# Up-projection of two ConvFFN layers: pairs of weight tiles by seven half-size products instead of eight, with sums of inputs and weights, and down groups added by DMA

## The chip, the cores and the metric

The kernel runs on one core of a Trainium2 chip. The metric is the device time of one execution in microseconds (us), lower is better. The engines are PE (TensorE), DVE (VectorE), ACT (ScalarE), POOL (GpSimd) and SP (SyncE, which issues DMA transfers). Each engine works through a row of instructions of its own, in a fixed order, and an instruction that waits holds up all that stands behind it in its row.

## The reference

Two layers over 528 tokens (16 meta tokens and 512 of the input) with 1024 features: sparse attention in the first, differential attention in the second, and after each a gated ConvFFN. The change lies in the ConvFFN:

```python
def conv_ffn(h, w_up, conv_w, conv_b, w_down):
    Tp = h.shape[1]
    u = h @ w_up
    up = jnp.pad(u, ((0, 0), (CONV_W - 1, 0), (0, 0)))
    c = conv_b + sum(up[:, j:j + Tp] * conv_w[j] for j in range(CONV_W))
    gate, val = jnp.split(c, 2, axis=-1)
    return (jax.nn.silu(gate) * val) @ w_down
...
h = h + conv_ffn(rms_norm(h, ln_ffn_g[i]), w_up[i], conv_w[i], conv_b[i], w_down[i])
```

`w_up` is 1024 x 5632 and `w_down` is 2816 x 1024. The 2816 columns of the gate and of the value half make 22 tiles of 128 each.

## The kernel before

Activations lie transposed, features on partitions and tokens along the row. Every fp32 product is made of three matmuls on numbers split into a high and a low part (fp32r): high by high, high by low, low by high. So a weight tile of 1024 x 128 arrives by DMA as `raw`, ACT casts it to `hi` (L111), and DVE (or POOL) subtracts to get `lo` (L113). The class `Weights` keeps one stream of such units, with three buffers each of `raw`, `hi` and `lo`; a unit's buffers come free when its matmuls are done.

`ffn(l)` runs over the tile pairs f = 0 to 21. For each f it makes the gate tile (e = 0) and the value tile (e = 1) with `lin`: 8 blocks of 128 features, two halves of the tokens (272 and 256; 260 and 256 in the second layer), three matmuls each, 48 matmuls to a tile, into one of two wide PSUM buffers (tag `sp`, two banks each). `evac` then does the convolution: ACT writes the first tap plus bias (L1065), DVE adds the two others (L1068, twice), ACT takes silu of the gate (L1073), DVE multiplies with the value (L1074), and ACT and DVE split the product into `ah` and `al` (L1077, L1078).

After pairs 6, 12 and 17 and at the end, `down` multiplies the finished act tiles with `w_down`, in eight groups (one for each 128 output features), and DVE adds each group's PSUM to the residual `h` (L1116). The order of instructions on each engine is set by a scheduler from the order of the code, the dependences and its own estimates.

Of the kernel before, what the change touches and what calls it, by code (L numbers as in the profile page):

```python
# [66 lines left out]
class Weights:  # L67
# [1 line left out]

    RAW = 3
    RING = 3

    def __init__(self, nc, pool, par):
        self.nc, self.pool, self.par = nc, pool, par
        self.units, self.loads, self.raw, self.out = [], [], {}, {}
        self.loaded = self.scaled = self.ready = self.taken = self.freed = 0
        self.held = 0

    def add(self, src, n=8, m=128, g=None, lo="v", fold=None):
        self.units.append((n, m, lo))
        self.loads.append((src, n, m, g, fold))

    def load(self):
        src, n, m, g, fold = self.loads[self.loaded]
        raw = self.pool.tile([128, 8, 128], F32, tag="raw", name="raw", bufs=self.RAW)
        dst = raw[:, :n, :m]
        self.nc.sync.dma_start(dst if fold is None else dst.rearrange("p (a k) c -> p a k c", a=fold), src)
        self.raw[self.loaded] = raw  # L90
        self.loaded += 1

    def scale(self):
        src, n, m, g, fold = self.loads[self.scaled]
        if g is not None:
            r = self.raw[self.scaled][:, :n, :m]
            self.nc.gpsimd.tensor_tensor(r, r, self.par[:, g:g + n, None].to_broadcast([128, n, m]), op=OP.mult)  # L97
        self.scaled += 1

    def split(self):  # L100
        nc = self.nc
        n, m, lo = self.units[self.ready]
        raw = self.raw.pop(self.ready)
        self.freed += 1
        r = raw[:, :n, :m]
        hi = self.pool.tile([128, 8, 128], F32R, tag="hi", name="hi", bufs=self.RING)
        lt = self.pool.tile([128, 8, 128], F32R, tag="lo", name="lo", bufs=self.RING)
        if lo == "pp":
            nc.gpsimd.tensor_scalar(hi[:, :n, :m], r, 1.0, 1.0, op0=OP.mult, op1=OP.mult)
        else:  # L110
            nc.scalar.copy(hi[:, :n, :m], r)  # L111
        eng = nc.vector if lo == "v" else nc.gpsimd
        eng.tensor_tensor(lt[:, :n, :m], r, hi[:, :n, :m].bitcast(F32), op=OP.subtract)  # L113
        self.out[self.ready] = (hi, lt)
        self.held += 1
        self.ready += 1

    def can_split(self):
        return self.ready < self.scaled and self.held < self.RING

    def pump(self, stop=None):
        while stop is None or self.ready < stop:
            if self.loaded < min(len(self.loads), self.freed + self.RAW):
                self.load()
            elif self.scaled < self.loaded:
                self.scale()
            elif self.can_split():
                self.split()
            else:
                return  # L130

    def take(self):
# [6 lines left out]
        return w  # L139

    def done(self):
        self.held -= 1
        self.pump()


# [4 lines left out]
class Trunk:  # L150
# [76 lines left out]
    def lin(self, x, evac, n=8, m=128, start=0, halves=(0, 1), w=None, kw=0, kx=0, done=True, tag="sp"):  # L227
# [9 lines left out]
        if done:  # L237
            self.wt.done()

    def halves(self, name):  # L240
        return tuple(self.ps.tile([128, 512], F32, tag="one", name=name) for _ in range(2))

# [9 lines left out]
    def setup(self):  # L252
# [15 lines left out]
        self.wt = Weights(nc, self.W, par)  # L268
        self.plan_weights()
        def part(s, k):  # L270
            c = slice(HO[s], HO[s] + HN[s])
# [60 lines left out]
    PW = ((0,0),(0,1),(1,0))  # L332

    def plan_ffn(self, l):
        wu, wd = self.a["w_up"][l], self.a["w_down"][l]
        for f in range(NF):
            for e in range(2):
                self.wt.add(wu[f + NF * e], lo=('p' if (f, e) in self.PW else 'v'))
            for f0, f1 in self.PARTS:
                if f == (f1 if f1 < NF else NF - 1):  # L340
                    for m in range(KC):
                        self.wt.add(wd[m][:, f0:f1, :], n=f1 - f0, lo="vv"[m % 2])

    def table(self, func, after=None):

# [133 lines left out]
    def norm(self, tmp, s, dst, g=None, start=0, gap=1.0, keep=None, lo="vp"):  # L479
# [23 lines left out]
        def apply(r):  # L503
            R = ps.tile([128, 512], F32, tag="one", name="R")
            for c in range(nt):
                i = nc.tensor.transpose(R[:, c * w:(c + 1) * w], r[:w, 8 + 2 * c:9 + 2 * c].to_broadcast([w, 128]),
                                        self.ident[:w, :w])
            self.hold(i)
            self.pe(0.107 * nt)
            dst[s] = self.xtile(s)  # L510
            xh, xl = dst[s][:2]
            o = c0 - HO[s]
            xfs, self.mults, self.his = [], [], []

            def low(m):
                eng = nc.vector if lo[m % len(lo)] == "v" else nc.gpsimd
                i = eng.tensor_tensor(xl[:, m, o:o + n], xfs[m][:, :n], xh[:, m, o:o + n].bitcast(F32),  # L517
                                      op=OP.subtract)
                if eng is nc.vector:
                    chain(i)  # L520

            last = [None]
# [527 lines left out]
    def ffn(self, l):  # L1050
# [1 line left out]
        st0 = 0 if l == 0 else 12  # L1052
        t0 = 0 if l == 0 else NM
        n = T - t0
        wt, x = self.wt, self.next_x
        cb = C_CONV + l * 176
        cnt = [0]
        self.xx, self.tm = ("ah", 8), ("c1", 2)
        with self.pool("fp") as fp:
            acts, conv = {}, {}  # L1060
            def evac(u, f, e, off=240):
                j = f + NF * e
                w0, w1, w2, b = (par[:, cb + 44 * q + j:cb + 44 * q + j + 1] for q in range(4))
# [24 lines left out]
            self.run(self.lin_many(x, first[2:], 0))  # L1088
            for j, (out, *_) in enumerate(first):
                if isinstance(out, tuple):  # L1090
                    u = fp.tile([128, T], F32, tag="uv", name="u", bufs=2)
# [25 lines left out]
                    if squares:  # L1117
                        self.norm_sum(fp, int(c0 == 272), m)

            def down(f0, f1):  # L1120
                last = f1 == NF
                squares = last and l == 0
                nf = f1 - f0

                def new():
                    cnt[0] += 1
                    if cnt[0] % 2:
                        t = ps.tile([128, 1024], F32, tag="sp", name="dn")
                    elif l == 1:
                        t = ps.tile([128, 512], F32, tag="one", name="dn")  # L1130
                    else:
                        t = self.halves("dn")
                    return t, wt.take()

                groups = [(0, 1), (2,), (3,), (4,), (5,), (6, 7)] if last else [(m,) for m in range(KC)]
                for grp in groups:
                    tw = [new() for _ in grp]
# [7 lines left out]
                    for ci, cc in enumerate(passes):  # L1145
# [2 lines left out]
                                block(t, w, f0 + k, k, cc, k == 0, k == nf - 1)  # L1148
                        for (t, w), m in zip(tw, grp):
                            add(t, m, cc, squares)  # L1150
                            if l == 1 and last:
# [10 lines left out]

            if l == 0:
                self.next_x = [None, None]
            for f in range(1, NF):
                for e in range(2):
                    if (f, e) != (1, 0):
                        self.run(self.lin(x, lambda u, f=f, e=e: evac(u, f, e), start=st0, tag="sp"))
                for f0, f1 in self.PARTS[:-1]:
                    if f == f1:  # L1170
                        down(f0, f1)
            if l == 0:
                self.table(AF.Sqrt, conv[0][:, 0:1])
            down(*self.PARTS[-1])
            self.flush()

# [469 lines left out]
```

## Time and profile before

| what | us |
|---|---|
| median of 3 runs (1385.61 to 1390.95) | 1386.35 |
| the profiled execution: its own time | 1384.77 |
| the profiled execution: span | 1383.0 |

| engine | busy us | share of the span |
|---|---|---|
| PE matmul | 1324.3 | 96% |
| PE weight load | 1278.4 | 92% |
| DVE | 852.2 | 62% |
| ACT | 589.3 | 43% |
| POOL | 286.2 | 21% |

The span runs from the first to the last instruction. Busy time overlaps across engines. Matmuls are pipelined: the duration of one (some 0.29 us) is longer than the distance between the starts of two (some 0.12 us), so the distances are what counts. The first ConvFFN lies at about 277 to 640 us, the second at about 1006 to 1383 us.

### The profile page before, as it was taken

How to read it: one execution, taken by the hardware profiler on the slowest of the kernel's cores; microseconds unless marked ns; L12 is line 12 of the kernel's file. 1: busy time of each engine (PE TensorE's matmuls, PEld its weight loads, DVE VectorE, ACT ScalarE, POOL GpSimd, SP SyncE). 2: the span in 40 equal slices, each digit the busy share in tenths (PEclk: the TensorE clock that was granted, in tenths of full speed). 3: DMA queues.
4: the chain of work that ended last, by engine and by line, in shares of the span. 5: the costliest groups of instructions: out<-in, count | busy, mean ns of one | idle time of the engine just before them, and what ended most of it. 6: DMA issues, size and time to landing. Idle time of an engine off the chain costs nothing.

```text
span 1383.0 us, 25034 instructions
## 1 busy us (share of the span) xinstructions
PE 1324.3 (96%) x10072; PEld 1278.4 (92%) x10072; DVE 852.2 (62%) x1734; ACT 589.3 (43%) x1114; POOL 286.2 (21%) x334
## 2 busy tenths in 40 slices
PE   5999899999999999999799999989899999999998
PEld 4999789899999999999799999989799899899897
DVE  6499977665445445555756767775755445545453
ACT  4453555554224333234435555655544234333231
POOL 3514533400000000002554533444500000000000
PEclk9999989999999999999999989999999999999999
DMA  7412222122332232323223222212222332332422
GB/s 233 118 48 89 84 70 80 61 78 81 88 95 82 85 107 69 106 83 89 73 80 85 79 66 64 72 48 69 77 62 84 93 109 85 88 107 64 121 71 97
DMA packets 46995, 118.98 MB, mean 86 GB/s; under 512 B 5936, under 2 KB 15456, under 8 KB 46880
## 3 DMA queue, kind: packets, MB, share of 16 engines
q1 hardware_dynamic: 46128, 114.57, 27.8%
q0 software_dynamic: 752, 2.82, 0.7%
q8 instruction: 79, 1.29, 0.4%
q14 instruction: 36, 0.29, 0.1%
HBM read 112.46 MB, written 4.91 MB: 85 GB/s over the span
## 4 chain that ended last, share of the span: by engine, by line
PE 84%; DVE 8%; ACT 2%; issue 2%; POOL 2%; DMA 1%; SPq 0%; POOLq 0%; DVEq 0%; ACTq 0%
PE lin L222 56%; PE dn L1105 17%; PE pv L1005 1%; PE stq L567 1%; PE pv L1453 1%; DVE lo L113 1%; PE sa L910 1%; DVE acc L447 1%; ACT hi L111 1%; PE linh L222 1%; DVE xl L517 1%; PE pt L1014 1%; PE stk L557 1%; PE pt L1467 1%; PE sb L1379 1%
## 5 line engine op out<-in xcount | busy, mean ns | idle before, releaser
L222 PE MATMUL lin<-xh,hi 128*128 128x256 f32 (+3 forms) x2208 | 635.0, 289 | 12.7 <-DVE ht L434 7.0
L222 PE MATMUL lin<-xl,hi 128*128 128x256 f32 (+3 forms) x2208 | 634.1, 287 | 2.4 <-POOL xl L517 1.8
L222 PE MATMUL lin<-xh,lo 128*128 128x256 f32 (+3 forms) x2208 | 634.5, 288 | 0.0
L222 PEld LDWEIGHTS lin<-xh,hi 128*128 128x128 f32 (+1 forms) x2208 | 420.6, 191 | 16.3 <-ACT xh L542 5.0
L222 PEld LDWEIGHTS lin<-xl,hi 128*128 128x128 f32 (+1 forms) x2208 | 421.5, 191 | 4.3 <-POOL xl L517 2.2
L222 PEld LDWEIGHTS lin<-xh,lo 128*128 128x128 f32 (+1 forms) x2208 | 421.6, 191 | 0.1
L111 ACT CAST hi<-raw 128x1024 fp32r<-128x1024 f32 (+3 forms) x209 | 199.4, 956 | 332.3 <-PE lin L222 167.0
L113 DVE TENSOR_TENSOR lo<-raw,hi 128x1024 fp32r<-128x1024 f32 (+3 forms) x180 | 201.9, 1123 | 223.1 <-ACT hi L111 222.7
L1105 PE MATMUL dn<-ah,hi 128*128 128x256 f32 (+2 forms) x528 | 142.3, 322 | 0.5 <-DVE ht L1116 0.5
L1105 PE MATMUL dn<-al,hi 128*128 128x256 f32 (+2 forms) x528 | 142.5, 321 | 0.0
L1105 PE MATMUL dn<-ah,lo 128*128 128x256 f32 (+2 forms) x528 | 141.9, 321 | 0.0
L1068 DVE SCALAR_TENSOR_TENSOR c<-lin,par,c 128x512 f32<-128x512 f32 (+2 forms) x172 | 129.7, 755 | 2.9
L1116 DVE TENSOR_TENSOR ht<-dn,ht 128x256 f32<-128x256 f32 (+2 forms) x96 | 46.6, 514 | 116.3 <-PE dn L1105 116.3
L1105 PEld LDWEIGHTS dn<-ah,hi 128*128 128x128 f32 x528 | 88.9, 188 | 9.0 <-DVE ht L1116 0.8
L1105 PEld LDWEIGHTS dn<-ah,lo 128*128 128x128 f32 x528 | 88.9, 188 | 7.8
L1105 PEld LDWEIGHTS dn<-al,hi 128*128 128x128 f32 x528 | 89.0, 188 | 7.4
L447 POOL TENSOR_TENSOR acc<-acc,nsq 128x256 f32<-128x256 f32 (+2 forms) x18 | 16.6, 929 | 378.2 <-PE dn L1105 360.7
L113 POOL TENSOR_TENSOR lo<-raw,hi 128x1024 fp32r<-128x1024 f32 (+1 forms) x31 | 70.3, 2268 | 64.7 <-ACT hi L111 64.3
L1077 ACT CAST ah<-c 128x528 fp32r<-128x528 f32 (+1 forms) x44 | 27.6, 627 | 102.9 <-DVE c L1074 102.9
L1065 ACT ACTIVATE c<-lin,par 128x528 f32<-128x528 f32 (+1 forms) x86 | 67.2, 781 | 0.0
L1073 ACT ACTIVATE c<-c 128x528 f32<-128x528 f32 (+1 forms) x44 | 28.1, 639 | 83.7 <-DVE c L1068 83.7
L97 POOL TENSOR_TENSOR raw<-raw,par 128x1024 f32<-128x1024 f32 x24 | 47.3, 1971 | 69.1 <-DMA raw<-w_kv 34.7
(255 smaller groups left out, 1760.8 us busy)
## 6 DMA issues: line engine op xcount, KB each, us to landing
raw<-w_up SPq DMA_DIRECT2D x88, 512.0 KB, 3.5
raw<-w_down SPq DMA_DIRECT2D x32, 384.0 KB, 3.1
raw<-w_down SPq DMA_DIRECT2D x32, 320.0 KB, 2.9
raw<-w_in SPq DMA_DIRECT2D x16, 512.0 KB, 3.6
raw<-w_kv SPq DMA_DIRECT2D x16, 512.0 KB, 3.7
nb<-nbias SPq DMA_DIRECT2D x16, 264.0 KB, 2.7
raw<-w_o_a SPq DMA_DIRECT2D x8, 512.0 KB, 3.6
raw<-w_q SPq DMA_DIRECT2D x8, 512.0 KB, 3.5
```

Source lines behind the costliest of these rows:

```text
L97: self.nc.gpsimd.tensor_tensor(r, r, self.par[:, g:g + n, None].to_broadcast([128, n, m]), op=OP.mult)
L111: nc.scalar.copy(hi[:, :n, :m], r)
L113: eng.tensor_tensor(lt[:, :n, :m], r, hi[:, :n, :m].bitcast(F32), op=OP.subtract)
L222: i = self.nc.tensor.matmul(o, w[wi][:, kw + k, :m], x[s][xi][:, kx + k, c0:HN[s]], start=(first and p == 0), stop=(last and p == 2))
L447: eng.tensor_tensor(acc, acc, sq[:, :n], op=OP.add)
L517: i = eng.tensor_tensor(xl[:, m, o:o + n], xfs[m][:, :n], xh[:, m, o:o + n].bitcast(F32), op=OP.subtract)
L1065: nc.scalar.activation(t[:, :n], u[:, off + t0:off + T], AF.Identity, bias=b, scale=w2)
L1068: nc.vector.scalar_tensor_tensor(t[:, z:n], u[:, off + t0 + z - d:off + T - d], w, t[:, z:n], op0=OP.mult, op1=OP.add)
L1073: nc.scalar.activation(c[:, :n], c[:, :n], AF.Silu)
L1077: nc.scalar.copy(ah[:, :n], c[:, :n])
L1105: nc.tensor.matmul(part(t, c0, c1, o), w[wi][:, k, :], acts[f][ai][:, c0:c1], start=(first and p == 0), stop=(last and p == 2))
L1116: nc.vector.tensor_tensor(hv, part(t, c0, c1, o), hv, op=OP.add)
```

## The change

Pairs f = 2 to 21 of each layer are computed as a 2 x 2 by 2 x 2 block product with seven products of blocks instead of eight (a Strassen-Winograd scheme). The blocks are gate and value (two output tiles), the two halves of the 1024 features, and the two halves of the tokens (264 each; 258 in the second layer). A product is 12 matmuls (4 feature blocks, three each). `up_pair` orders them so that they accumulate in the two PSUM tiles `g` and `v`, with two copies by ACT (L1233, L1236) and two additions by DVE (L1242, L1255) between them.

- Sums of weights: for each pair DVE makes four sums of half tiles (`Weights.sum`, L135 to L140), and ACT and DVE split the two sum tiles `S12` and `S34` besides the gate tile and half of the value tile: 28 feature blocks of weights instead of 16.
- Sums of the input, once in each layer: PE adds and subtracts input blocks in PSUM with the identity and its negative as weights (48 matmuls), and ACT and DVE split the result (`TT`).
- Down: four groups of four act tiles (`PARTS`) and a tail of six; the weights of the groups and half of the value tile come through a second stream (`wsm`, its own three buffers of half size). A group's PSUM is copied by ACT (L1350) and added to `h` by a DMA with accumulation, issued from POOL (L1351). The tail is added by DVE as before.

```diff
-    def __init__(self, nc, pool, par):
+    def __init__(self, nc, pool, par, depth=8, tag="", ring=3):
...
+    def sum(self):
+        p, half = divmod(self.summed, 2)
...
+        t = self.extra.tile([128, 8, 128], F32, tag=kind, name=kind, bufs=1)
+        gw, vw = g["raw"], v["raw"]
+        add = self.nc.vector.tensor_tensor
+        if half == 0:
+            add(t[:, 0:4], vw[:, 0:4], vw[:, 4:8], op=OP.add)
+            add(t[:, 4:8], t[:, 0:4], gw[:, 0:4], op=OP.subtract)
+            self.s2 = t[:, 4:8]
+        else:
+            add(t[:, 4:8], gw[:, 4:8], self.s2, op=OP.subtract)
+            add(t[:, 0:4], gw[:, 0:4], vw[:, 0:4], op=OP.subtract)
...
-    PARTS = ((0, 6), (6, 12), (12, 17), (17, 22))
+    PLAIN = 2
+    PARTS = ((0, 4), (4, 8), (8, 12), (12, 16))
+    TAIL = 16
...
+        for f in range(self.PLAIN, NF):
+            g, v = (wt.load_of(wu[f + NF * e]) for e in range(2))
+            wt.unit("raw", g)
+            pair = wt.pair(g, v)
+            wt.unit("S12", pair)
+            wt.unit("S34", pair)
...
+            ws.unit("raw", v, 4, 4)
...
+            def product(out, w, wk, xs, xk, c0, first=True):
+                for k in range(4):
+                    for p, (wi, xi) in enumerate(((0, 0), (0, 1), (1, 0))):
+                        nc.tensor.matmul(out, w[wi][:, wk + k, :], xs[xi][:, xk + k, c0:c0 + N],
...
+            def up_pair(f):
...
+                G, S12 = wt.take(), wt.take()
+                product(g0, G, 0, x0, 0, st0)
...
+                nc.scalar.copy(v0, g0)
+                product(g1, S12, 0, TT[0], 0, 0)
+                p5 = fp.tile([128, 264], F32, tag="p", name="p5", bufs=2)[:, :N]
+                nc.scalar.copy(p5, g1)
...
+                product(v0, S12, 4, TT[1], 0, 0, False)
+                nc.vector.tensor_tensor(g1, v0, p5, op=OP.add)
+                if f + 1 < NF:
+                    wt.sum()
+                product(g0, G, 4, x0, 4, st0, False)
+                wt.done()
+                wt.done()
...
+                S34 = wt.take()
+                product(v0, S34, 0, TT[2], 0, 0, False)
+                nc.vector.tensor_tensor(v1, v0, p5, op=OP.add)
+                product(g1, S34, 4, x1, 4, mid - 264, False)
+                evac(g, f, 0, off)
...
+                A22 = ws.take()
+                product(v0, A22, 0, TT[3], 0, 0, False)
+                evac(v, f, 1, off)
...
+            def down(p, m):
+                f0, f1 = self.PARTS[p]
+                t, w = new(), ws.take()
+                for k in range(f1 - f0):
+                    if k == (f1 - f0) // 2:
+                        yield
+                    block(t, w, f0 + k, k, cols, k == 0, k == f1 - f0 - 1)
+                y = fp.tile([128, T], F32, tag="y", name="y", bufs=2)
+                for c0, c1, o in cols:
+                    nc.scalar.copy(y[:, c0:c1], part(t, c0, c1, o))
+                nc.gpsimd.dma_start(self.h[m][:, t0:T], y[:, :n], accum_op=OP.add)
+                yield
...
             for f in range(1, NF):
+                if f >= self.PLAIN:
+                    self.run(more)
+                    up_pair(f)
+                    continue
...
```

Three places show where instructions stand. The first is DVE in the first layer. Before, this is what DVE does for one whole pair of tiles (`lo` is the low part of the next weights, `c0` and `c1` the convolutions of gate and value):

```order
L113 TENSOR_TENSOR lo_3778<-raw_3644,hi_3777 128x1024
L1068 SCALAR_TENSOR_TENSOR c0_3773<-lin_3724,par_73,c0_3773 128x527
L1068 SCALAR_TENSOR_TENSOR c0_3773<-lin_3724,par_73,c0_3773 128x526
L113 TENSOR_TENSOR lo_3843<-raw_3657,hi_3842 128x1024
L1068 SCALAR_TENSOR_TENSOR c1_3832<-lin_3783,par_73,c1_3832 128x527
L1068 SCALAR_TENSOR_TENSOR c1_3832<-lin_3783,par_73,c1_3832 128x526
L1074 TENSOR_TENSOR c0_3773<-c0_3773,c1_3832 128x528
L1078 TENSOR_TENSOR al_3839<-c0_3773,ah_3838 128x528
```

In the change, DVE's row for pair f = 7 begins with the addition into `g_4687` (L1242) and a `lo` for the next gate tile; then follow the rows below, and after them the value's second tap, the product with silu and `al`:

```order
L167 TENSOR_TENSOR lo_4763<-S12_4743,hi_4762 128x1024
L1255 TENSOR_TENSOR v_4700<-v_4700,p5_4714 128x264
L135 TENSOR_TENSOR S12_4946<-raw_4791 128x512
L136 TENSOR_TENSOR S12_4946<-S12_4946,raw_4685 128x512
L167 TENSOR_TENSOR lo_4823<-S34_4788,hi_4822 128x1024
L1278 SCALAR_TENSOR_TENSOR c0_4818<-g_4687,par_73,c0_4818 128x527
L167 TENSOR_TENSOR lo_4986<-raw_4679,hi_4985 128x512
L139 TENSOR_TENSOR S34_4991<-raw_4685,S12_4946 128x512
L140 TENSOR_TENSOR S34_4991<-raw_4685,raw_4791 128x512
L1278 SCALAR_TENSOR_TENSOR c1_4852<-v_4700,par_73,c1_4852 128x527
L1278 SCALAR_TENSOR_TENSOR c0_4818<-g_4687,par_73,c0_4818 128x526
```

The gate's two taps (`c0_4818<-g_4687`) used to follow each other right behind one `lo`; now the low part of the next pair's S34 weights stands ahead of the first, and a `lo` of down weights, two sums and the value's first tap stand between the first and the second.

The second place is ACT for the same pair. Before:

```order
L111 CAST hi_3718<-raw_3628 128x1024
L1065 ACTIVATE c1_3708<-lin_3659,par_73 128x528
L1077 CAST ah_3714<-c0_3649 128x528
L111 CAST hi_3777<-raw_3644 128x1024
L1065 ACTIVATE c0_3773<-lin_3724,par_73 128x528
```

and now, from the copy of the gate's first product to the copy for the next pair:

```order
L1233 COPY v_4700<-g_4687 128x264
L1236 COPY p5_4714<-g_4687 128x264
L165 CAST hi_4758<-raw_4482 128x1024
L165 CAST hi_4762<-S12_4743 128x1024
L165 CAST hi_4822<-S34_4788 128x1024
L1275 ACTIVATE c0_4818<-g_4687,par_73 128x528
L165 CAST hi_4985<-raw_4679 128x512
L1275 ACTIVATE c1_4852<-v_4700,par_73 128x528
L1283 ACTIVATE c0_4818<-c0_4818 128x528
L1287 CAST ah_4858<-c0_4818 128x528
L1233 COPY v_4903<-g_4890 128x264
```

Three casts of weights for the next pair stand ahead of the gate's first tap (L1275), and the copy for the next pair (the last row) stands behind this pair's silu and `ah`.

The third place is PE, where one pair ends and the next begins, with what a row waits for in brackets. Before (the last matmuls of one tile and the first of the next):

```order
L222 MATMUL lin_4031<-xh1_3351,hi_3901 128x256
L222 MATMUL lin_4031<-xl1_3352,hi_3901 128x256
L222 MATMUL lin_4031<-xh1_3351,lo_3902 128x256
L222 MATMUL lin_4096<-xh0_3478,hi_3966 128x272 [waits DVE_49,Activation_49]
L222 MATMUL lin_4096<-xl0_3479,hi_3966 128x272
```

and now (the end of the first product of pair f = 7, six matmuls `dn` of a down group, and the start of the second product):

```order
L1213 MATMUL g_4687<-xl0_3497,hi_4555 128x264
L1213 MATMUL g_4687<-xh0_3496,lo_4556 128x264
L1316 MATMUL dn_5030<-ah_4655,hi_4878 128x256 [waits Activation_49]
L1316 MATMUL dn_5029<-ah_4655,hi_4878 128x272
L1316 MATMUL dn_5030<-al_4656,hi_4878 128x256 [waits DVE_49]
L1316 MATMUL dn_5029<-al_4656,hi_4878 128x272
L1316 MATMUL dn_5030<-ah_4655,lo_4879 128x256
L1316 MATMUL dn_5029<-ah_4655,lo_4879 128x272
L1213 MATMUL g_4687<-Th0_3425,hi_4559 128x264 [waits Activation_49]
```

The down matmuls, which stood in blocks of whole groups between the pairs, now stand inside the pairs, and those here wait for `ah_4655` and `al_4656`, the act tile of the pair just before. The counts of down matmuls from pair to pair are 22, 80, 72 and 18, and so on in turns of four pairs.

## Rows read from the trace of the kernel before

**Rows 1.** The page: busy time and share of each engine, and the granted clock

```profile
PE 1324.3 (96%) x10072; PEld 1278.4 (92%) x10072; DVE 852.2 (62%) x1734; ACT 589.3 (43%) x1114; POOL 286.2 (21%) x334
PEclk9999989999999999999999989999999999999999
```

**Rows 2.** The page: the chain that ended last

```profile
PE 84%; DVE 8%; ACT 2%; issue 2%; POOL 2%; DMA 1%; SPq 0%; POOLq 0%; DVEq 0%; ACTq 0%
```

**Rows 3.** Busy time by stretch: from:to, sum, then PE, PEld, DVE, ACT, POOL, clock, DMA share, GB/s

```profile
300.14:346.94 46.80, 46.80 (x384) 46.80 (x384) 27.01 (x32) 18.86 (x26) 0.00 (x0) 1.00 0.28 83
1041.20:1086.60 45.40, 45.40 (x381) 45.23 (x380) 26.14 (x33) 18.24 (x25) 0.00 (x0) 1.00 0.27 79
```

**Rows 4.** ACT in order of time, first layer: start, us, instruction [idle before <-releaser]

```profile
299.19 1.05 ACT L111 CAST hi<-raw 128x1024 fp32r<-128x1024 f32 x1 [1.05 <-PE lin L222]
300.14 0.79 ACT L1065 ACTIVATE c<-lin,par 128x528 f32<-128x528 f32 x1
303.81 0.63 ACT L1077 CAST ah<-c 128x528 fp32r<-128x528 f32 x1 [2.88 <-DVE c L1074]
...
308.94 0.65 ACT L1073 ACTIVATE c<-c 128x528 f32<-128x528 f32 x1 [2.14 <-DVE c L1068]
310.94 1.05 ACT L111 CAST hi<-raw 128x1024 fp32r<-128x1024 f32 x1 [1.35 <-PE lin L222]
```

**Rows 5.** DVE in order of time, first layer, one pair

```profile
300.27 1.22 DVE L113 TENSOR_TENSOR lo<-raw,hi 128x1024 fp32r<-128x1024 f32 x1 [1.40 <-ACT hi L111]
301.42 1.56 DVE L1068 SCALAR_TENSOR_TENSOR c<-lin,par,c 128x527 f32<-128x527 f32 x2
303.01 0.71 DVE L1074 TENSOR_TENSOR c<-c,c 128x528 f32<-128x528 f32 x1
304.48 0.71 DVE L1078 TENSOR_TENSOR al<-c,ah 128x528 fp32r<-128x528 f32 x1 [0.76 <-ACT ah L1077]
```

**Rows 6.** DVE in order of time, second layer: start and a pair

```profile
1025.12 0.74 DVE L1068 SCALAR_TENSOR_TENSOR c<-lin,par,c 128x512 f32<-128x512 f32 x1
1025.78 0.74 DVE L1068 SCALAR_TENSOR_TENSOR c<-u,par,c 128x512 f32<-128x512 f32 x1
...
1041.22 1.22 DVE L113 TENSOR_TENSOR lo<-raw,hi 128x1024 fp32r<-128x1024 f32 x1 [3.02 <-ACT hi L111]
...
1064.02 1.23 DVE L113 TENSOR_TENSOR lo<-raw,hi 128x1024 fp32r<-128x1024 f32 x1 [3.01 <-ACT hi L111]
```

**Rows 7.** Groups by form: DVE and ACT instructions of nearly the new sizes

```profile
L1078 DVE TENSOR_TENSOR al<-c,ah 128x512 fp32r<-128x512 f32 x22 | 15.2, 691 | 13.3 <-ACT ah L1077 13.3
L1116 DVE TENSOR_TENSOR ht<-dn,ht 128x256 f32<-128x256 f32 x32 | 13.4, 422 | 56.1 <-PE dn L1105 56.1
L1471 ACT CAST ph<-pt 128x256 fp32r<-128x256 f32 x40 | 14.3, 364 | 7.2 <-PE pt L1467 6.4 <-PE pv L1453 0.4
```

**Rows 8.** DVE in order of time, start of the first layer's pairs

```profile
289.31 1.23 DVE L113 TENSOR_TENSOR lo<-raw,hi 128x1024 fp32r<-128x1024 f32 x1 [5.98 <-ACT hi L111]
```

**Rows 9.** DMA issues: KB each, median us from issue to landing

```profile
nbias<-brow POOLq DMA_DIRECT2D x1, 572.0 KB, 10.5
nbias<-big POOLq DMA_DIRECT2D x1, 128.0 KB, 3.5
```

**Rows 10.** PE in order of time around a wait in differential attention

```profile
713.82 1.14 PE L589 MATMUL Rk<-ident,ex 88*128 88x88 f32 x6 [2.15 <-POOL ex L584]
...
715.06 0.43 PE L222 MATMUL lin<-xl,hi 128*128 128x272 f32 x1
715.28 0.43 PE L222 MATMUL lin<-xh,lo 128*128 128x272 f32 x1
...
719.43 0.28 PE L222 MATMUL lin<-xh,hi 128*128 128x256 f32 x1
```

**Rows 11.** PE in order of time: the longest wait near the first pairs

```profile
293.17 0.36 PE L222 MATMUL lin<-xh,hi 128*128 128x272 f32 x1 [1.46 <-DVE c L1068]
293.37 0.28 PE L222 MATMUL lin<-xl,hi 128*128 128x272 f32 x1
```

More of the change, by code (lines that the diff above doesn't have):

```diff
@@ L67 @@
 class Weights:
-    RAW = 3
-    RING = 3
-    def __init__(self, nc, pool, par):
[L76 to L79, printed above, removed]
-    def add(self, src, n=8, m=128, g=None, lo="v", fold=None):
-        self.units.append((n, m, lo))
-        self.loads.append((src, n, m, g, fold))
-    def load(self):
[L86 to L90, printed above, removed]
+    def __init__(self, nc, pool, par, depth=8, tag="", ring=3):
+        self.nc, self.pool, self.par, self.depth, self.tag, self.ring = nc, pool, par, depth, tag, ring
+        self.loads, self.units, self.pairs, self.out, self.sums = [], [], [], {}, {}
+        self.loaded = self.scaled = self.summed = self.ready = self.taken = self.finished = 0
+        self.extra, self.peer, self.ends, self.end = None, None, [], 1 << 30
@@ new lines, in add, with tile, can_load @@
+    def add(self, src, n=8, m=128, g=None, lo="v", fold=None):
+        self.unit("raw", self.load_of(src, n, m, g, fold), 0, n, m, lo)
+    def tile(self, dt, name):
+        return self.pool.tile([128, self.depth, 128], dt, tag=name + self.tag, name=name, bufs=self.ring)
+    def can_load(self):
+        i = self.loaded
+        return i < min(len(self.loads), self.end) and self.pool is not None and (i < self.ring or not self.loads[i - self.ring]["reads"])
+    def load(self):
+        d = self.loads[self.loaded]
+        d["raw"] = self.tile(F32, "raw")
+        dst, f = d["raw"][:, :d["n"], :d["m"]], d["fold"]
+        self.nc.sync.dma_start(dst if f is None else dst.rearrange("p (a k) c -> p a k c", a=f), d["src"])
@@ L91, in load @@
         self.loaded += 1
     def scale(self):
-        src, n, m, g, fold = self.loads[self.scaled]
+        d = self.loads[self.scaled]
+        g, n, m = d["g"], d["n"], d["m"]
         if g is not None:
-            r = self.raw[self.scaled][:, :n, :m]
+            r = d["raw"][:, :n, :m]
             self.nc.gpsimd.tensor_tensor(r, r, self.par[:, g:g + n, None].to_broadcast([128, n, m]), op=OP.mult)
+        d["ok"] = True
         self.scaled += 1
+    def sum(self):
+        p, half = divmod(self.summed, 2)
+        g, v = self.pairs[p]
+        kind = ("S12", "S34")[half]
+        assert g["ok"] and v["ok"] and kind not in self.sums, "no weights to sum up"
+        t = self.extra.tile([128, 8, 128], F32, tag=kind, name=kind, bufs=1)
[8 more added lines that the diff above has]
+            add(t[:, 0:4], gw[:, 0:4], vw[:, 0:4], op=OP.subtract)
+        for r in (g, v):
+            r["reads"] -= 1
+        self.sums[kind] = t
+        self.summed += 1
+        self.pump()
@@ L121, in pump @@
     def pump(self, stop=None):
         while stop is None or self.ready < stop:
[L123 to L129, printed above, removed]
+            if not self.step() and not (stop is None and self.peer is not None and self.peer.step()):
                 return
@@ L141, in done @@
     def done(self):
-        self.held -= 1
+        self.finished += 1
         self.pump()
@@ L238, in lin, with beside @@
             self.wt.done()
+    @staticmethod
+    def beside(main, more):
+        for _ in main:
+            yield
+            next(more, None)
     def halves(self, name):
@@ L520, in low @@
                     chain(i)
+                    self.low = i
             last = [None]
@@ L1164, in ffn @@
                 self.next_x = [None, None]
+            at_late, at_mid = self.down_slots()
+            with self.tc.issue_after(self.low.ins):
+                wt.sum()
+                wt.sum()
             for f in range(1, NF):
+                if f >= self.PLAIN:
+                    self.run(more)
+                    up_pair(f)
+                    continue
                 for e in range(2):
                     if (f, e) != (1, 0):
[L1168 to L1171, printed above, removed]
+                        self.run(self.beside(self.lin(x, lambda u, f=f, e=e: evac(u, f, e), start=st0, tag="sp"), more))
             if l == 0:
                 self.table(AF.Sqrt, conv[0][:, 0:1])
-            down(*self.PARTS[-1])
+            down_last(self.TAIL, NF)
             self.flush()
+            wt.extra = ws.pool = None
     def mixer_b(self):
```

191 lines of the change are left out of this document (153 added, 38 removed).

## Prediction

> **What bounds the kernel now.** I read the engines' shares first, then the chain that ended last, then the stretches with the pairs. PE is busy for 96% of the span, DVE for 62% [rows 1], and 84% of the chain is PE [rows 2]. In four pairs of the first layer PE works 46.8 of 46.8 us at full granted clock; DVE works 27.0 us there, in the second layer 26.1 of 45.4 [rows 3]. So a pair costs what its matmuls cost: ACT's casts of two neighbouring pairs start at 299.19 and 310.94, 11.75 us apart [rows 4], which over 96 matmuls is 0.1223 us each. In the second layer two pairs take 1041.22 to 1064.02 [rows 6], 11.40 us each, 0.1188 a matmul. The reader is to see that ACT and DVE wait for PE (idle before them: "<-PE lin", [rows 4]) and that DVE has 42% of each pair in hand.
>
> **The change part by part.**
>
> Removed: 12 matmuls a pair. 20 pairs x 12 x 0.1223 = 29.4 us and 20 x 12 x 0.1188 = 28.5 us, together 57.9. Added on PE: 48 matmuls for the input sums in each layer, 5.9 + 5.7 = 11.6. If PE stayed the bound: 1384.8 - 57.9 + 11.6 = 1338.5. The down matmuls are as many as before.
>
> The new DVE work, with prices: `lo` of a whole weight tile 1.15 (300.27 to 301.42, start to start), a dependent pair of taps 1.56, the product with silu and `al` 0.71 each [rows 5]; a half tile of weights, as `lo` or as a sum, 0.62, an estimate between 0.69 (`al` of 512 columns, visible length [rows 7]) and half of the whole tile's 1.15; a tap with another instruction between 0.68 (1025.12 to 1025.78 are 0.66 apart [rows 6]); the addition into `g` or `v` 0.42 (`ht<-dn`, 256 columns [rows 7]). A sum of two SBUF tiles has no row; from below 0.58, from above 0.78 (a dependent tap, half of 1.56). Per pair: three whole `lo`, one half, four sums, two additions, four taps, product and `al`: 3.45 + 0.62 + 2.48 + 0.84 + 2.84 + 1.42 = 11.7, and about one more for the down weights (32 half tiles in 20 pairs): 12.7. PE's share of a pair becomes 84 x 0.1223 = 10.27, with the down matmuls (on average 48 x 0.1223 = 5.9 a pair while groups last) 16.1. So DVE's total would fit on average, but not in a pair without down work. What decides is the order.
>
> The order makes a ring. The gate tile `g` and the value tile `v` fill both PSUM buffers of tag `sp`. The first product of the next pair overwrites `g`, so it waits for the gate's second tap. In DVE's row that tap stands behind `lo` of the next S34, which needs ACT's cast, which needs a free weight buffer, which comes with the end of the pair's sixth product (g1 by S34). After it PE has only the seventh product and whatever down matmuls stand there. Before, the other buffer's tile, a whole one of 48 matmuls, lay over the convolution.
>
> I walk from T0, the end of the third product (v0 by S12), first layer; a product is 12 x 0.1223 = 1.47. DVE's addition into `g1` ends at 0.75 (about 0.2 to start, 0.42, 0.1 back: handoffs are estimates). Three products end at 5.15. ACT's cast of S34 (1.05 [rows 4]) ends at 6.3, DVE's `lo` (1.15) at 7.45. Then gate tap 0.68, half `lo` 0.62, two sums 1.24, value's tap 0.68, the gate's second tap 0.76: 11.45. The next first product starts at 11.55 and ends at 13.0. Then 0.6 to 1.1 for what stands ahead of the second product: the copy of `v0`, which on ACT stands behind silu and `ah` (0.65 and 0.63 [rows 4]), and down matmuls that wait for the act tile of the pair just before. Two products more: T0 again at 16.5. PE is idle from 6.6 (end of the seventh product) to 11.5 less the down matmuls there.
>
> With down matmuls, by turns of four pairs:
> - 22 of them: 17.1.
> - 80: PE-bound, (84 + 80) x 0.1223 = 20.0, taken as 20.1.
> - 72: 19.1 of work, 19.7.
> - 18: 18.5, since 12 lie ahead of the ring's wait and six behind it, which wait for `al`.
>
> One turn is 75.4, where four pairs and 192 down matmuls took 4 x 11.75 + 192 x 0.1223 = 70.5. The pairs 2 to 21 make 19 intervals: 17.8 (the first, 12 down matmuls) + 3 x 75.4 + 56.9 (17.1 + 20.1 + 19.7) + 46.4 (the last three without down work: 16.5, 15.9 and 14.0, as there is less to split) = 347, where before 19 x 11.75 + 768 x 0.1223 = 317.2. That is +30.
>
> The start of each layer: ahead of T0 of pair 2 DVE must do 8 half-tile sums (5.0), four whole and three half `lo` (4.6 + 1.9), taps of the two plain pairs (8 x 0.72), 16 splits of the input sums (6.4 at 0.4) and four products or `al` (2.8), 26.3 us, of which the hole of 5.98 us that DVE has there [rows 8] takes some. I put T0 of pair 2 at 9.5 us later than the removed matmuls alone would have it; 5.9 of that are the 48 matmuls. Bounds: 5.9 if all DVE work is hidden, 14 if half a hole only. So +40 in the first layer. In the second, PE's steps are 3% shorter and DVE's as long: +41 by the same walk. Sum at full clock: 1384.8 + 81 = 1466.
>
> The additions into `h` by DMA: a group's PSUM is now emptied by ACT (some 0.4 + 0.4, by the cast of 256 columns at 0.364 [rows 7]) where DVE needed 0.42 + 0.42, and a transfer of 264 KB goes out from POOL, which has nothing else in these stretches [rows 3]. It matters only if it lands later than the group after next wants its `y` buffer. Nearest rows on POOL's queue: 3.5 us for 128 KB, 10.5 us for 572 KB [rows 9]; between them by size 5.6. Two groups are at least 48 x 0.1223 = 5.9 apart and mostly some 15: nothing, and 10.5 in the worst case is a rival. The Trainium skill ("DMA: Bandwidth & Descriptors", section Anatomy of one DMA — SWDGE path) gives about 2.0 us plus the bytes by 436 GB/s, an estimate of 2.6 us here; both rows are above that rule (2.3 and 3.3 us by it), so I keep the rows.
>
> PE's clock: in differential attention a wait of 2.15 us ended at 713.82, and the linear's matmuls behind it still started 0.22 apart (715.06, 715.28) and were 0.43 long, until one was 0.28 long at 719.43 [rows 10], where 0.122 is the pace of the pairs at full clock. That is 1.2 instead of 2.4 GHz for at least 4.4 us, and a loss of 4.4 x (1 - 0.122 / 0.22) = 2.0. A wait of 1.46 us (ended 293.17) left the second matmul behind it 0.28 long [rows 11]; I count it as no fall. The walk has seven idles of over 4 us in a layer (three at the 18-interval, four without down work or nearly): 14 x 2.0 = 28. Bounds: 0 (no fall, since the matmuls around are dense) and 22 idles, 44. Taking 28: 1494, and the median of the runs shown is 1.6 above the profiled execution: 1495.
>
> **The rivals.**
>
> *PE stays the bound* (the other side). The walk may put too much ahead of the gate's second tap: if the ring of weight buffers frees early, so that S34's cast does not come last, the tap ends by 9 and the average interval falls. It decides at the point where an interval is under (317.2 - 9.9) / 19 = 16.2 us on average (9.9: the start of 9.5 and a handoff), against 18.3 walked; at PE's own pace it is (19 x 10.27 + 768 x 0.1223) / 19 = 15.2. With all cover kept the time is 1338.5, with the start's 3.6 us on each layer 1345. For it: DVE's sum 12.7 is under 16.1. Against it: four waits in a row (PE to ACT to DVE to PE), each with work in front. The Trainium skill ("Perfetto Trace Analysis", section Identifying the Most-Contended Engine) says to optimize the engine of highest occupancy, by weight loads for TensorE; by that rule the change takes work from the right engine (weight loads 92%, DVE 62% [rows 1]) and should come out so.
>
> *Waits without the clock.* The same ring, but idles broken up by the seventh product and the first leave the clock up: 1466, from 1440 (half of the intervals' excess hidden) to 1480.
>
> *The DMA adds land late.* At 10.5 us each, ACT's copies wait for `y`, and with them the next pair's casts. Some 1.5 us for each of 64 groups: 96 on top, 1590. Against it: the rows' own 5.6 by size.
>
> *No net change.* The waits eat just the gain: each interval 2 us shorter than walked, 1380 to 1392.
>
> **How the numbers follow.** Waits with falls of the clock 0.55 (1475 to 1530), waits alone 0.25, late adds 0.04, PE-bound 0.12, no change 0.04. 0.5%, about 7 us, is about what a measurement of this kernel can tell from no change. The likeliest is 1495. The range leaves out the last three cases (0.20): its low end is the walk with half of its excess (81 / 2) and no fall, 1425; its high end 1466 with 44 for the clock, 9 for the start at its bound and 0.7 more of handoffs in each of the 38 intervals, 1545. Faster 0.12, same 0.04, slower 0.84.
>
> **What would show it.** In the profile after: PE's share well under 96% and DVE's over 62%; in the pairs idle of 3 to 5 us ahead of the first product (L1213), ended by the gate's tap (DVE, L1278), in two of four pairs; intervals of 20 us at PE's full rate where 80 or 72 down matmuls stand; ACT's cast of S34 ended by PE and `lo` directly ahead of the gate's tap; granted clock under 1.00 behind the long idles; DMA landing of `h<-y` under 6 us. Wrong if DVE stands idle while PE works at 100% between pairs, if the idle ahead of the first product is under 1 us, or if the next S34's `lo` is long done when the sixth product ends.

## The result, and the profile after

The changed kernel takes 1513.66 us (median of 4 runs, 1511.91 to 1522.66), the kernel before 1386.18. The ratio is 1.0924, with a 95% interval of 1.0874 to 1.0975: 9% slower, where 1495 (1425 to 1545) was forecast. The ratios below, and the medians of these two kernels, leave out two slow executions: 3156.99 us of "All taps first" and 1589.77 us of "Cover alone", which is the one that was profiled there.

The page of the profiled execution (span 1510.1 us): busy time of the engines, granted clock in 40 slices, the chain that ended last, and the landing time of the accumulating DMAs.

```profile
PE 1342.5 (89%) x9688; PEld 1272.9 (84%) x9688; DVE 1031.8 (68%) x2030; ACT 726.4 (48%) x1426; POOL 343.1 (23%) x398
...
PEclk9999899989999999979899999889899999999989
...
PE 69%; DVE 18%; ACT 5%; issue 4%; DMA 3%; POOL 1%; SPq 0%; DVEq 0%; ACTq 0%; POOLq 0%
...
ht<-y POOLq DMA_DIRECT2D x32, 264.0 KB, 5.3
...
ht<-y POOLq DMA_DIRECT2D x32, 256.0 KB, 4.9
```

PE has 384 instructions fewer than before and is busy for 18 us *longer* [rows 1]: many of its matmuls ran at half clock. Its share of the chain fell from 84% to 69% [rows 2], DVE's rose from 8% to 18%.

Where the time went shows in three stretches (first ConvFFN, differential attention, second ConvFFN; each ends with the last addition into `h`). Columns: the stretch, its length, PE, PE's weight loads, DVE, ACT and POOL busy, granted clock, DMA share, GB/s. Before:

```profile
271.60:666.70 395.10, 390.62 (x3177) 389.45 (x3175) 216.34 (x300) 143.19 (x198) 21.43 (x16) 1.00 0.30 88
666.70:999.70 333.00, 312.12 (x2455) 304.39 (x2455) 231.53 (x642) 178.98 (x441) 158.68 (x191) 0.94 0.24 70
999.70:1379.20 379.50, 377.34 (x2641) 353.08 (x2641) 199.23 (x261) 131.65 (x177) 3.83 (x5) 0.99 0.30 90
```

and after:

```profile
272.90:726.60 453.70, 397.16 (x2986) 385.98 (x2984) 303.32 (x437) 211.88 (x370) 49.47 (x48) 0.94 0.37 96
726.60:1067.00 340.40, 317.17 (x2455) 309.77 (x2455) 235.21 (x642) 179.46 (x442) 158.78 (x191) 0.93 0.23 69
1067.00:1506.30 439.30, 383.12 (x2449) 344.74 (x2449) 288.12 (x419) 199.68 (x317) 32.45 (x37) 0.95 0.37 97
```

The two ConvFFNs grew by 58.6 and 59.8 us, differential attention, which no edit touches, by 7.4, the rest by 1.3: 127 in all. What the half clock cost is PE's busy time by what the clock lacks of 1.00: 397 x 0.06 + 383 x 0.05 = 43 us in the ConvFFNs, 4 before. The clock has two digits there; in stretches of 2 us the same sum gives 41 and 6, so 35 of the 118 us are clock and 83 are waits and added work.

What PE waited for, over the whole kernel (total, times, longest):

```profile
PE g L1213 <- DVE c L1278: 67.8, 26, 4.7
...
PE g L1213 <- DVE g L1242: 10.0, 16, 1.0
PE dn L1316 <- DVE lo L167: 9.3, 14, 1.0
PE dn L1316 <- ACT hi L165: 8.4, 12, 0.8
```

The first row is the first product of a pair waiting for a convolution tap of the pair before. One such wait, in order of time: ACT, then DVE, then PE (start, duration, instruction, idle before it and what ended it).

```profile
398.25 1.05 ACT L165 CAST hi<-S 128x1024 fp32r<-128x1024 f32 x1 [1.87 <-PE g L1213]
399.20 0.78 ACT L1275 ACTIVATE c<-g,par 128x528 f32<-128x528 f32 x1
```

```profile
399.33 1.22 DVE L167 TENSOR_TENSOR lo<-S,hi 128x1024 fp32r<-128x1024 f32 x1
400.47 0.76 DVE L1278 SCALAR_TENSOR_TENSOR c<-g,par,c 128x527 f32<-128x527 f32 x1
401.15 0.68 DVE L167 TENSOR_TENSOR lo<-raw,hi 128x512 fp32r<-128x512 f32 x1
401.75 0.68 DVE L139 TENSOR_TENSOR S<-raw,S 128x512 f32<-128x512 f32 x1
402.35 0.68 DVE L140 TENSOR_TENSOR S<-raw 128x512 f32<-128x512 f32 x1
402.95 0.76 DVE L1278 SCALAR_TENSOR_TENSOR c<-v,par,c 128x527 f32<-128x527 f32 x1
403.63 0.75 DVE L1278 SCALAR_TENSOR_TENSOR c<-g,par,c 128x526 f32<-128x526 f32 x1
```

```profile
404.53 0.56 PE L1213 MATMUL g<-xh,hi 128*128 128x264 f32 x1 [4.74 <-DVE c L1278]
404.89 0.42 PE L1213 MATMUL g<-xl,hi 128*128 128x264 f32 x1
405.11 0.42 PE L1213 MATMUL g<-xh,lo 128*128 128x264 f32 x1
```

The cast of the next S34 starts as soon as PE has ended the sixth product (398.2); the gate's second tap, the seventh DVE instruction behind it, ends at 404.4. PE is idle for 4.74 us, and behind that its matmuls start 0.22 apart, the half clock of [rows 10].

### The profile page after: what moved, and what is told of

Its sections match the earlier page's. It is cut to its first block, busy times and chain, and to the rows that moved or that the text cites. A ratio compares the mean times of both kernels' runs of the same rounds, so it can differ in the third digit from the quotient of the medians.

```text
span 1510.1 us, 25344 instructions
## 1 busy us (share of the span) xinstructions
PE 1342.5 (89%) x9688; PEld 1272.9 (84%) x9688; DVE 1031.8 (68%) x2030; ACT 726.4 (48%) x1426; POOL 343.1 (23%) x398
## 4 chain that ended last, share of the span: by engine, by line
PE 69%; DVE 18%; ACT 5%; issue 4%; DMA 3%; POOL 1%; SPq 0%; DVEq 0%; ACTq 0%; POOLq 0%
PE lin L279 21%; PE g L1213 15%; PE dn L1316 13%; PE v L1213 8%; DVE c L1278 4%; DVE lo L167 4%; ACT hi L165 3%; DMA raw<-w_up 2%; PE stq L654 1%; DVE S L139 1%; PE pv L1681 1%; PE pv L1092 1%; DVE S L140 1%; PE linh L279 1%; PE sa L997 1%
## 5 line engine op out<-in xcount | busy, mean ns | idle before, releaser
L279 PE MATMUL lin<-xh,hi 128*128 128x256 f32 (+3 forms) x928 | 274.1, 300 | 12.5 <-DVE ht L520 7.1
L279 PE MATMUL lin<-xl,hi 128*128 128x256 f32 (+3 forms) x928 | 273.9, 296 | 3.1 <-DVE xl L603 2.8
L165 ACT CAST hi<-raw 128x512 fp32r<-128x512 f32 (+3 forms) x225 | 184.0, 823 | 191.2 <-PE dn L1316 70.9
L279 PE MATMUL lin<-xh,lo 128*128 128x256 f32 (+3 forms) x928 | 273.7, 296 | 0.0
L167 DVE TENSOR_TENSOR lo<-raw,hi 128x512 fp32r<-128x512 f32 (+3 forms) x196 | 180.6, 930 | 74.6 <-ACT hi L165 72.3
L1213 PE MATMUL g<-xh,hi 128*128 128x264 f32 (+1 forms) x480 | 147.3, 307 | 77.8 <-DVE c L1278 67.8
L1351 POOL DMA_DIRECT2D ht<-y x64 | 55.9, 874 | 615.5 <-ACT y L1350 603.1
L279 PEld LDWEIGHTS lin<-xh,hi 128*128 128x128 f32 (+1 forms) x928 | 181.4, 197 | 16.2 <-ACT xh L629 7.4
L279 PEld LDWEIGHTS lin<-xl,hi 128*128 128x128 f32 (+1 forms) x928 | 182.9, 197 | 4.7 <-DVE xl L603 4.3
L279 PEld LDWEIGHTS lin<-xh,lo 128*128 128x128 f32 (+1 forms) x928 | 182.6, 197 | 0.1
L1213 PE MATMUL g<-xh,lo 128*128 128x264 f32 (+1 forms) x480 | 142.7, 297 | 0.0
```

What stands on the lines that cost most here:

```text
L165: nc.scalar.copy(hi[:, :n, :m], src)
L167: eng.tensor_tensor(lt[:, :n, :m], src, hi[:, :n, :m].bitcast(F32), op=OP.subtract)
L279: i = self.nc.tensor.matmul(o, w[wi][:, kw + k, :m], x[s][xi][:, kx + k, c0:HN[s]], start=(first and p == 0), stop=(last and p == 2))
L1213: nc.tensor.matmul(out, w[wi][:, wk + k, :], xs[xi][:, xk + k, c0:c0 + N], start=(first and k == 0 and p == 0), stop=(k == 3 and p == 2), ...
L1351: nc.gpsimd.dma_start(self.h[m][:, t0:T], y[:, :n], accum_op=OP.add)
```

## The experiments

The theory: the loss is the order of work, a gate's second tap that comes late, with the half clock behind the idles that it makes. One rival, "load": DVE's 12.7 us a pair are the bound wherever they stand. Another: the down groups by ACT and DMA, or the split streams, cost time of their own.

### One edit each

**The next S34 weights behind the gate's taps.** An ordering edge puts their cast behind the gate's first tap on ACT and their low part behind the second tap on DVE.

```diff
-                wt.done()
+                with self.tc.issue_after(self.tap.ins), self.tc.issue_after(self.first.ins):
+                    wt.done()
...
```

> The cast and the low part of the next S34 weights are queued behind the gate's first tap (ACT) and its second tap (DVE); no work is added or left out. Theory order (the gate's second tap comes late because of what stands ahead of it): the first product of the next pair starts some 2.5 to 3 us after the end of the sixth product instead of 7.5, the light intervals fall from 17 to 19.2 us to 13.5 to 15, the long idles that bring the half clock vanish: 1415 to 1440 us. Theory load (12.7 us of DVE work a pair are the bound, wherever they stand): within 10 us of 1514.

1452.15 us, ratio 1.0485 (1.0453 to 1.0517): 61 us off with the same work (DVE 2030 instructions as in the change, busy 1033.4 us where it was 1031.8), so order and not load; but less than forecast. PE's two waits in one pair:

```profile
474.09 0.36 PE L1213 MATMUL g<-xh,hi 128*128 128x264 f32 x1 [1.12 <-DVE c L1281]
...
478.76 0.39 PE L1213 MATMUL g<-Th,hi 128*128 128x264 f32 x1 [2.97 <-ACT v L1233]
```

The first wait fell from 4.74 to 1.12 us, and a new one of 2.97 came behind the first product: ACT's copy into the next value tile, which stood until the value's second tap had read the old one. That tap now was the late one (ACT and DVE):

```profile
477.47 0.76 DVE L1281 SCALAR_TENSOR_TENSOR c<-v,par,c 128x526 f32<-128x526 f32 x1
```

```profile
478.34 0.36 ACT L1233 COPY v<-g 128x264 f32<-128x264 f32 x1 [3.32 <-DVE c L1281]
```

**Matmuls in the idle.** Matmuls with an unused result fill the idle ahead of the first products of pairs 20 and 21; they wait for nothing.

```diff
...
+                    m = 34 if f == 20 else 22
+                    with self.tc.issue_after(self.last.ins):
+                        for k in range(m):
+                            i = nc.tensor.matmul(t, x0[0][:, k % 4, 16:144], x1[0][:, k % 4, 0:256], start=(k == 0), stop=(k == m - 1))
+                    with self.tc.issue_after(i.ins):
+                        product(g0, G, 0, x0, 0, st0)
...
```

> 34 and 22 matmuls of 256 columns into a spare PSUM bank, whose result nothing reads, stand in the idle ahead of the first products of pairs 20 and 21 in each layer; the order of all else is as in the change. Theory clock (the idle itself brings the half clock): the products behind those two idles start 0.12 apart instead of 0.22, four times 2 us less, 1504 to 1507 us. Rival (the clock falls for another reason, the idle only lies beside it): 0.22 apart still, 1514 or a little above.

1494.68 us, ratio 1.0802 (1.0775 to 1.0829). The 4.5 us from the two first products on, in the change and here (columns as in the stretches above):

```profile
657.00:661.50 4.50, 3.99 (x16) 3.69 (x17) 1.94 (x3) 1.59 (x3) 0.00 (x0) 0.50 0.32 87
675.80:680.30 4.50, 3.99 (x20) 3.68 (x21) 1.94 (x3) 1.59 (x3) 0.00 (x0) 0.59 0.02 4
```

```profile
655.50:660.00 4.50, 3.85 (x29) 3.64 (x30) 1.94 (x3) 1.88 (x4) 0.00 (x0) 1.00 0.32 87
670.65:675.15 4.50, 3.86 (x29) 3.66 (x30) 1.95 (x3) 1.89 (x4) 0.00 (x0) 1.00 0.00 0
```

With the idle filled the clock stays at 2.4 GHz, and 29 matmuls start in the time of 16 to 20: the idle brings the fall. In the traces the two ConvFFNs are 6.3 and 2.6 us shorter, 8.9 where 8 was forecast; the other 9 of the 18 us between the two traces lie in differential attention (7.7) and other stages without an edit.

**Sums of weights on POOL.**

```diff
-        add = self.nc.vector.tensor_tensor
+        add = self.nc.gpsimd.tensor_tensor
```

> The four half-tile sums of weights of each pair go from DVE to POOL. Theory order: the long idles lose the two sums that stand between the gate's taps, 1.2 us of 4.7 each, the low part of S34 stays ahead: 1485 to 1500. Theory load: 2.4 us less DVE work in each of 40 pairs, some 95 us off: about 1420.

1504.81 us, ratio 1.0856 (1.0818 to 1.0895): order was too hopeful by 5 to 20 us. For load this is a weak test, since DVE's busy time fell by 35 us (1031.8 to 997.1) and not by the 95 of the sums; but the 9 us that it gave are too few for it even so. DVE and POOL at one pair:

```profile
1177.12 2.21 DVE L167 TENSOR_TENSOR lo<-S,hi 128x1024 fp32r<-128x1024 f32 x1 [1.31 <-ACT hi L165]
...
1179.91 1.30 DVE L167 TENSOR_TENSOR lo<-raw,hi 128x512 fp32r<-128x512 f32 x1
```

```profile
1176.97 1.28 POOL L136 TENSOR_TENSOR S<-S,raw 128x512 f32<-128x512 f32 x1
1179.40 1.26 POOL L140 TENSOR_TENSOR S<-raw 128x512 f32<-128x512 f32 x1 [1.16 <-DVE lo L167]
```

A `lo` that takes 1.22 us took 2.21 beside a POOL sum, a half one 1.30 instead of 0.68: DVE seems to have stood until the sum ended (1178.25) and then worked for its own 1.1. The Trainium skill ("SBUF — State Buffer", section SBUF: two separate sides) says that DVE with two SBUF inputs and GpSimd hold a shared pair of ports exclusively for a whole instruction; these rows agree. So the sums left DVE's row and came back, in part, as waits in it.

**Eight products.** The second stream, groups of four and accumulating DMAs stay; sums, copies and additions go.

```diff
...
-                product(g0, G, 0, x0, 0, st0)
...
-                product(v0, A22, 0, TT[3], 0, 0, False)
+                for k in (0, 4):
+                    product(g0, G, k, x0, k, st0, k == 0)
+                for k in (0, 4):
+                    product(g1, G, k, x1, k, mid - 264, k == 0)
...
+                for k in (0, 4):
+                    product(v0, V, k, x0, k, st0, k == 0)
+                for k in (0, 4):
+                    product(v1, V, k, x1, k, mid - 264, k == 0)
...
```

> Pairs 2 to 21 by eight products of half size (96 matmuls, no sums of weights or inputs, no copies or additions between products), with the second stream for the down weights, the groups of four and the accumulating DMAs as in the change. Theories order and load, both of which put the loss on the seven products: 1386 to 1400 (some 7 us of it in differential attention, which takes that much longer in the change). Rival (the down groups by ACT and DMA or the split streams cost time by themselves): over 1420.

1385.07 us, ratio 1.0002 (0.9982 to 1.0022): everything in the change but the seven products costs nothing that can be measured. Differential attention took 335 us, so the 7 us that I had added for it were not there.

### The change again, and edits together

**The change, unaltered.**

> The change, unaltered, on the chip of the three kernels below. Differential attention, which no edit touches, took 7 us longer in the first profile of the change than in the kernel before and in the other experiments. If that was one execution, its stretch takes 333 us here and the median comes to 1505 or so; if the change brings it about, 340 us and 1513.

1509.78 us, ratio 1.0889 (1.0835 to 1.0942). Differential attention took 337.2 us here, between the two answers. In the other kernels it takes 331.5 to 336.2, so some of the 7 us is one execution's, and whether the change adds a little stays open.

**All taps first.** The S34 sums and the half-tile low parts go behind the value's second tap as well.

```diff
...
                evac(v, f, 1, off)
+                with self.tc.issue_after(self.tap.ins):
+                    if f + 1 < NF:
+                        wt.sum()
+                    wt.pump()
...
```

> As the experiment that puts the gate's taps ahead of the S34 weights, and besides that the two S34 sums and the half-tile low parts come behind the value's taps, since the copy into the next value tile waited 3 us for the value's second tap there. Theory order: that wait falls from 3 us to about 1, light intervals of 13.2 to 14.5 us, less half clock: 1410 to 1435. Theory load (DVE's work in a light pair, 12.7 us and a wait or two, is what is left): no better than the 1452 of the first.

1412.30 us, ratio 1.0192 (1.0152 to 1.0232), as the theory had it: 101 us of the 127 (97 against the change on the same chip) are gone by order alone, with every instruction of the change still there. The clock's loss in the ConvFFNs (summed in stretches of 2 us) is 10 us, of 41. The two ConvFFNs (columns as above):

```profile
272.80:684.60 411.80, 380.14 (x2985) 371.94 (x2983) 302.83 (x436) 211.15 (x370) 49.44 (x48) 0.98 0.39 105
1016.50:1405.40 388.90, 364.28 (x2449) 330.75 (x2449) 287.96 (x421) 198.81 (x317) 32.34 (x37) 0.99 0.40 110
```

The scheduler also spread the down matmuls anew: 36, 24, 75 and 57 from pair to pair in the first layer, where the change has 18, 22, 80 and 72. How much of the 101 us that spread brings is not shown; the next experiment has a spread of its own with the taps left late.

**Cover alone.** DVE keeps the change's order; of the 48 down matmuls of a pair, 24 are pinned between its seventh product and the next pair's first, 24 behind that first product.

```diff
...
+                with self.tc.issue_after(self.last.ins) if f > self.PLAIN else nullcontext():
+                    product(g0, G, 0, x0, 0, st0)
+                a = at_mid.get(f)
+                a = a and down(*a)
+                if a:
+                    with self.tc.issue_after(self.last.ins):
+                        next(a)
+                        next(a)
...
```

> DVE's order is the change's; the down matmuls are pinned, 24 between the seventh product and the next pair's first and 24 behind that first product, in each pair from 4 or 5 to 20. The chain from the sixth product to the gate's second tap still decides: 5.15 + 6.4 + 1.47 + 2.94 + 2.94 = 18.9 us for each interval where the change has 19.6 on average, and no half clock in them: 1475 to 1495. If the loss lay in the uneven spread of the down matmuls alone (theory load in a pair without them), 16.2 us each and 1390.

1576.84 us, ratio 1.1349 (1.1289 to 1.1410): 82 us above the forecast and slower than the change, where faster was forecast. PE's waits ahead of four first products, each with the row behind it:

```profile
438.73 0.56 PE L1215 MATMUL g<-xh,hi 128*128 128x264 f32 x1 [2.82 <-DVE c L1283]
439.08 0.42 PE L1215 MATMUL g<-xl,hi 128*128 128x264 f32 x1
...
460.00 0.36 PE L1215 MATMUL g<-xh,hi 128*128 128x264 f32 x1 [2.75 <-DVE c L1283]
460.20 0.28 PE L1215 MATMUL g<-xl,hi 128*128 128x264 f32 x1
...
480.01 0.56 PE L1215 MATMUL g<-xh,hi 128*128 128x264 f32 x1 [2.81 <-DVE c L1283]
480.37 0.42 PE L1215 MATMUL g<-xl,hi 128*128 128x264 f32 x1
...
609.48 0.56 PE L1215 MATMUL g<-xh,hi 128*128 128x264 f32 x1 [2.70 <-DVE c L1283]
609.83 0.42 PE L1215 MATMUL g<-xl,hi 128*128 128x264 f32 x1
```

The chain did decide: 19.9 us from pair to pair where the clock held (the second of the four), 1 us over the forecast. But an idle of 2.6 to 2.9 us, in the second layer of 2.9 to 3.6, now stands in every pair with down matmuls, not one of 4.7 in every fourth, and behind most of them the clock fell: in the profiled execution, which is 13 us longer than the median, the clock's loss in the ConvFFNs is 90 us, of which I had counted none.

**Both.**

> Both edits, all taps first and the down matmuls pinned. Theory order: 16.2 us of PE work and 0.6 us for the addition into g, 16.8 us an interval, full clock, 1380 to 1400. Theory load: DVE's 12.7 us a pair are under 16.8, so it expects the same here.

1398.33 us, ratio 1.0095 (1.0059 to 1.0131), and 16.9 to 17.3 us from pair to pair with down matmuls in the first layer: as forecast. The largest wait left in the pairs (total, times, longest) is the one for DVE's addition into `g`:

```profile
PE g L1215 <- DVE g L1250: 28.8, 40, 1.6
```

**The cover split.** Half of the 24 matmuls behind the first product move behind the third.

```diff
...
                    with self.tc.issue_after(self.last.ins):
                        next(a)
-                        next(a)
...
                product(v0, S12, 4, TT[1], 0, 0, False)
+                gap = self.last
+                if a:
+                    with self.tc.issue_after(gap.ins):
+                        next(a)
...
```

> As the kernel with all taps first and the down matmuls pinned, but the 24 behind the next pair's first product are halved, and the second 12 stand behind the third product, where PE waited 0.6 to 1.0 us for DVE's addition into g in each of 17 intervals a layer. Theory order (the rest of the loss is this wait): 16.2 to 16.4 us an interval, 34 times 0.65 = 22 us less, 1376. Rival (the wait comes back as one for the copy into v, which now has 12 matmuls ahead of it and not 24): 1390 to 1398.

1374.00 us, ratio 0.9914 (0.9888 to 0.9941): 0.9% under the kernel before (1385.09 on the same chip), the first of these kernels that is faster. The intervals from pair 5 to pair 20 of the first layer are 16.1 to 16.9 us, the two ConvFFNs take 387 and 373 us, and the clock holds in them:

```profile
272.50:659.30 386.80, 370.90 (x2985) 364.83 (x2984) 301.22 (x437) 212.18 (x370) 49.74 (x48) 1.00 0.43 112
992.90:1365.90 373.00, 361.42 (x2450) 331.99 (x2449) 285.42 (x420) 198.99 (x317) 32.42 (x37) 0.99 0.44 114
```

**Pairs 2 and 3 by eight products.**

```diff
-    PLAIN = 2
+    PLAIN = 4
...
```

> The same, and pairs 2 and 3 by eight products as in the kernel before, since no down matmuls exist yet to stand in their idles: they took 13.6 us there with seven products and 11.75 by eight. 3.7 us less in each layer, and the start's 2 us of waits for the splits of the input sums hidden by more matmuls: 1364 to 1370. If the seven products pay in them after all (the idles only move to pair 4): as the one above.

1372.22 us, ratio 0.9914 (0.9881 to 0.9946): no better than the one above, as the rival had it. The second product of pair 4 starts 2.6 us earlier (333.07 instead of 335.70; 0.9 of it comes from ahead of the layer), but behind a wait, for ACT's copy into the value tile. That copy waited in turn for DVE's two taps of the value tile of pair 3, the last plain pair (PE, DVE, ACT):

```profile
333.07 0.39 PE L1215 MATMUL g<-Th,hi 128*128 128x264 f32 x1 [2.76 <-ACT v L1242]
```

```profile
330.99 1.56 DVE L1293 SCALAR_TENSOR_TENSOR c<-lin,par,c 128x527 f32<-128x527 f32 x2
```

```profile
332.66 0.36 ACT L1242 COPY v<-g 128x264 f32<-128x264 f32 x1 [2.15 <-DVE c L1293]
```

Behind the idle of 2.76 us the clock fell, and the pair's interval takes 17.1 us instead of 15.8: half clock again, 1.7 us by the sum used above.

## Why the prediction was right, and where it was off

**The ring.** The light interval was walked tap by tap, and the trace follows it: idle 4.9 us walked, 4.74 measured; half `lo` and sums at 0.62 each, 0.60 measured (401.15 to 401.75 to 402.35). From the second product of a pair to that of the next, which is as long as from T0 to T0, the change has in the first layer:

| down matmuls | walked, us | measured, us |
|---|---|---|
| 18 | 18.5 | 19.2 |
| 22 | 17.1 | 17.4 to 18.3 |
| 80 | 20.1 | 20.7 to 21.6 |
| 72 | 19.7 | 19.8 |
| a turn of four | 75.4 | 77.7 to 78.6 |

A turn's excess of 2.3 to 3.2 us is the half clock behind its long idle (2.9 us by the sum in stretches of 2 us), which the walk counted apart. One sign did not come: idles of 3 to 5 us ahead of the first product in two of four pairs. The trace has them in one of four; where 22 down matmuls stand PE waits some 3 us too, but in five pieces of 0.3 to 1.0 us. Moving the taps, with every instruction kept, took 101 us off: the order was the cause.

**The clock.** Counted 28, measured 35. The idles that were counted are there, seven in each layer: six of 4.1 to 4.75 us and one of 2.9. What was too small is the price. From the second product of pair 2 to that of pair 21 the clock cost 21 us in the first layer and 12 in the second, 2.4 us an idle and not 2.0; behind the idle shown above the matmuls stayed at half clock from 404.5 to 410.4, 5.9 us where the prediction had "at least 4.4" and counted just that. The runs show besides that idles of 2.7 to 2.8 us can bring a fall, though not each time.

**Waits and added work at full clock.** 81 walked, 83 measured, and that close a fit is partly luck. By layers it is 37 where 40 was walked and 46 where 41 was. In the first layer the 19 intervals fit (347 walked; 367.8 measured, 346.7 without the clock's 21.1), but the start, put at 9.5 us, cost about 7: the second product of pair 2 starts 37.8 us into the stretch, and the same place in the kernel before lies 32.3 us into it, 1.7 of them clock. The second layer was not walked by itself ("by the same walk"), and which of its terms is short stays open.

**What was left out.** The stages without an edit, 8.7 us in the profiled execution; part of it is one execution's.

**The rivals.** DMA adds landing late: 5.3 and 4.9 us, near the 5.6 worked out by size from [rows 9]; with eight products they cost nothing, and in the change ACT's copies waited for a landing four times, 1.4 us in all. These times are twice the 2.6 us that was estimated by the Trainium skill's rule ("DMA: Bandwidth & Descriptors", section Anatomy of one DMA — SWDGE (gpsimd) path). PE as the bound: not here. What spoke for it, that DVE's sum is under PE's, proved right as soon as the order was mended: then PE is nearly the bound, 1374 where the bound was 1338.5 to 1345; the rest is mostly the light pairs (13.6 us where PE works 10.3) and up to 0.7 us in most others.

## What to carry to other kernels

A saving on the busiest engine counts only if the chain round its buffers is shorter than the work that is left to cover it. Here each matmul taken out was cover for a convolution, and each sum put in stood ahead of it. So walk one period of the ring (last product, cast, low part, tap, next first product), put first on each engine what frees a buffer, then lay independent matmuls into what idle remains. A cover that only shortens every idle and closes none can cost more than none, since here the clock fell behind idles of 2.7 us as well.

## What had not been expected of the hardware

In the trace of "Cover alone" an idle of 2.75 us left the clock up, one of 2.81 us took it down 20 us later, and so did a shorter one of 2.70 us: length alone does not tell. And two engines got in each other's way though neither waited for the other's result: with the sums on POOL DVE's `lo` of S12 and S34 took 1.56 us on average, where it takes 1.22 without (80 instructions each); the longest took 2.25, one of 2.21 is shown above.
